# adaLN loads queued behind the weights' loads, and the attention masks built behind the layer's norm, in a four-stage decoder trunk

## The chip, the cores and the metric

One core of one Trainium2 chip runs the whole program. The metric is the device time in microseconds (us) of one execution; the profile is one execution of the same program, taken by the hardware profiler, and its span runs from the first to the last instruction. The engines are TensorE (PE, whose weight loads are listed as PEld), VectorE (DVE), ScalarE (ACT), GpSimd (POOL) and SyncE (SP, which here only issues DMAs).

## The reference

The trunk has two residual layers of 1024 tokens by 1024 channels, in float32. Each layer is a mixer and then a gated MLP with a causal convolution (ConvFFN), and each of these is preceded by an RMS norm that is shifted, scaled and gated from a conditioning vector `c` (adaLN):

```
cs = silu(c)
for i in range(2):
    sh_m, sc_m, g_m, sh_f, sc_f, g_f = split(cs @ ada_w[i] + ada_b[i], 6)
    hm = rms_norm(x, norm_mix[i]) * (1 + sc_m) + sh_m
    y = even_mixer(hm) if i == 0 else odd_mixer(hm)
    x = x + g_m * y
    hf = rms_norm(x, norm_ffn[i]) * (1 + sc_f) + sh_f
    x = x + g_f * conv_ffn(hf)
```

The even mixer is a gated DeltaNet in four heads beside a multi-scale pooling. The odd mixer is attention in three groups (dilations 1, 4 and 16) with eight heads each: `q`, `k` and `v` come from one projection, `q` and `k` are normed, and the scores get an ALiBi bias and a causal window before the softmax.

## The kernel before

All large products are made three times over: a float32 operand `a` is split into a rounded part `hi` (a cast on ACT, L193) and its rest `lo = a - hi` (a subtraction, L194), and TensorE adds up `hi*hi`, `hi*lo` and `lo*hi` (L220 to L222 and L1442 to L1444). `granule` (L196) does that for one 128x512 block of weights: an SP DMA into a `raw` tile (four buffers), the cast to `whi`, and the rest to `wlo` (nine buffers each). Who makes the rest is the variable `lo_eng`: GpSimd or VectorE. `last_w` holds the last weights' DMA traced so far.

The program is written as generators. A dense one (`dense`, `update`, `units`) yields matmuls; a chain of small work is woven into it (`weave`, L92) at given distances. The framework then lists the traced instructions on each engine: it puts first what was traced first among what is ready by its own plan, and an instruction whose buffer or input isn't free yet may be passed by later ones. `after(ins)` (L109) adds the condition that the block's instructions on the engine of `ins` come behind `ins` in that engine's queue; those on other engines are not bound. Each engine then runs its queue strictly in order, and SP issues its DMAs in order too.

The stages, in us of the profiled span: the even mixer until about 450, its output projection and the norm of the first ConvFFN until about 606; ConvFFN 0 until about 1216 (its up projection to about 950 by a Strassen scheme, `up`, one block of 128 gate and value columns at a time, with weights loaded as 512 KB `wr` tiles by `w_sums`, L1296; then the down projection, `update`); the attention layer until about 2250; ConvFFN 1 to the end.

The adaLN products are not made on TensorE, but for a few at the start: `ada_steps` (L274) loads one 128x512 block of `ada_w` at a time into a `raw` tile (L278), multiplies it by a column of `cs` and adds it up on DVE (L292, L294) or, in the down projection, on ACT and POOL (L288, L290). It is advanced one step at a time by `step_back` (L115), which `units`, `update` and `up` call behind their matmuls. Steps run only where `secs_due` lets them: from the third head of the even mixer on (L792), where sections 4 to 9 are made, and then in ConvFFN 0 from its fifth block on (L1353), where the other 14 follow; `sections(24)` (L1371) finishes the rest before the attention layer's norm vector.

The attention layer `odd` starts with the spill of `xt`, sets `lo_eng` to VectorE, builds the masks (`bm`, `bd`, from `rel` and `par`) and the vector `gq`, and then runs `dense`: `section(g, "v", hq)` loads the first eight granules of weights, and `tproj` multiplies them with the normed tokens, 256 at a time. At that point only the first half of the tokens is normed. The norm of the second half is woven into the first `tproj` (L1525): four transposes and a sum (`sums_of`, L328), the reciprocal root on DVE (`rsqrt`, L130), a broadcast by TensorE (`row_of`, L377), and then eight tiles scaled (L394), shifted (L403, L404), cast (L406) and split (L407; the even tiles' rest by GpSimd, the odd ones' by VectorE; `last_norm` is the last of them, on VectorE). The masks are first read by the attention's scores, `gq` by the first turn of `q` (L1485).

Of the kernel before, what the change touches and what calls it, by code (L numbers as in the profile page):

```python
# [13 lines left out]
ALU = mybir.AluOpType  # L14
# [3 lines left out]
P = 128  # L18
T = 1024
D = 1024  # L20
KT = D // P
TT = T // P
HALF = 512
# [11 lines left out]
def trunk(ctx, tc, x, c, ada_w, ada_b, norm_mix, norm_ffn, ev_w_in, ev_w_out, gdn_conv_w,  # L35
# [35 lines left out]
    def t2k():  # L71
        return tmp("t2k", [P, HALF], 8)
# [19 lines left out]
    def weave(chain, dense):  # L92
        for need in chain:
            if callable(need):
                while not need():
                    assert next(dense) is not None or need()
                continue
            t = 0.0
            while t < need:
                c = next(dense, None)  # L100
                if c is None:
                    break
                t += c
# [5 lines left out]
    def after(inst):  # L109
        return tc.issue_after(inst.ins) if inst is not None else nullcontext()  # L110
# [73 lines left out]
    def colv(name, i, n=1):  # L184
        a = col_at[name] + i
        return cols[:, a:a + n]
# [87 lines left out]
    def ada_steps(l, secs, raw_of):  # L274

        def load(s, k):
            raw = raw_of()
            nc.sync.dma_start(raw, ada_w[l].rearrange("(p k) n -> p k n", k=KT)[:, k, s * P:s * P + HALF])  # L278
            return raw

        for s in secs:
            acc = tmp("ada_acc", [P, HALF], 2, pl=pa[0])
            raw = load(s, 0)
            yield 1
            for k in range(KT):
                nxt = load(s, k + 1) if k < KT - 1 else None
                if by_pool[0]:
                    nc.scalar.activation(raw if k else acc, raw, AF.Copy, scale=cs[:, k:k + 1])  # L288
                    if k:
                        nc.gpsimd.tensor_tensor(out=acc, in0=acc, in1=raw, op=ALU.add)  # L290
                elif k == 0:
                    nc.vector.tensor_scalar(out=acc, in0=raw, scalar1=cs[:, 0:1], scalar2=None, op0=ALU.mult)  # L292
                else:
                    nc.vector.scalar_tensor_tensor(out=acc, in0=raw, scalar=cs[:, k:k + 1], in1=acc,  # L294
                                                   op0=ALU.mult, op1=ALU.add)
                raw = nxt
                yield 1
            ada_cols(l, s, acc)
            yield 1
# [1078 lines left out]
    def odd(xt, h, vec, acc):  # L1378
# [1 line left out]
        gate = mod[1][:, 16:24]  # L1380
        ready, res, qks, vss = set(), {}, {}, {}
        spill(xs[1], xt)
        lo_eng[0] = nc.vector
        with tc.tile_pool(name="po", bufs=1) as po:
            fill(po, 64)

            def et(tag, bufs, shape=(P, HALF), dt=F32):
                return tmp(tag, shape, bufs, dt, pl=po)


            bm = po.tile([P, 3, P], F32, name="bm")
            bd = po.tile([P, P], F32, name="bd")
            rel = t2k()[:, :P]
            nc.gpsimd.iota(rel, pattern=[[1, P]], base=0, channel_multiplier=-1,
                           allow_small_or_imprecise_dtypes=True)
            for i in (0, 2):
                nc.gpsimd.affine_select(out=bm[:, i, :], in_=rel, compare_op=GE, fill=NEG, base=0,
                                        pattern=[[-1, P]], channel_multiplier=1)
            par = po.tile([P, 2], F32, name="par")
            nc.vector.tensor_reduce(out=par, in_=ident.rearrange("p (m s) -> p s m", s=2), axis=mybir.AxisListType.X,  # L1400
                                    op=ALU.add)
            nc.vector.tensor_scalar(out=par, in0=par, scalar1=NEG, scalar2=None, op0=ALU.mult)
            for s in range(2):
                ev = "p (m s) -> p s m"
                nc.vector.tensor_scalar(out=bd.rearrange(ev, s=2)[:, s, :], in0=bm[:, 0, :].rearrange(ev, s=2)[:, s, :],
                                        scalar1=0.5, scalar2=par[:, 1 - s:2 - s], op0=ALU.mult, op1=ALU.add)
            nc.gpsimd.tensor_scalar(out=rel, in0=rel, scalar1=-float(P), scalar2=None, op0=ALU.add)
            nc.gpsimd.affine_select(out=bm[:, 1, :], in_=rel, compare_op=GE, fill=NEG, base=0,
                                    pattern=[[1, P]], channel_multiplier=-1)
            gq = po.tile([P, 1], F32, name="gq")  # L1410
            nc.vector.scalar_tensor_tensor(out=gq, in0=colv("att_q", 0), scalar=float(P) ** -0.5, in1=colv("att_k", 0),
                                           op0=ALU.mult, op1=ALU.mult)

            def tok_rows(d, g, blk):
                if g == 0:
# [6 lines left out]
            def section(g, kind, i):  # L1422

                base, out_ = g * 3072, []
                for k in range(KT):
                    rows = w[k * P:(k + 1) * P, :]
                    if kind == "v":
                        out_.append(granule(rows[:, base + 2048 + i * HALF:base + 2048 + (i + 1) * HALF]))
                    else:
                        out_.append(granule(rows[:, base:base + 2048].rearrange("p (s c) -> p s c", s=2)  # L1430
                                            [:, :, i * 256:(i + 1) * 256], ("p (s c) -> p s c", dict(s=2))))
                return out_
# [82 lines left out]
            def dense():  # L1515
                for i, (g, hp) in enumerate(todo):
                    while i >= 2 and ("att", i - 2) not in ready:
                        yield None
                    hq = hp // 2
                    if (g, hq) not in vd:  # L1520
                        wg = section(g, "v", hq)
                        for b2 in range(4):
                            gen = tproj(wg, b2)
                            if i == 0 and b2 == 0:
                                weave(norm(xt, vec, h, 1, acc, (1.8, 4.5)), gen)  # L1525
                            while True:
                                try:
                                    c = next(gen)
                                except StopIteration as e:
                                    ps = e.value  # L1530
                                    break
                                if turn:
                                    run_turn(1)
                                yield c
                            v = big(F32, "v")
                            nc.scalar.copy(v, ps)
                            if b2 == 0:
                                vd[(g, hq)] = dram.tile([T, HALF], F32, name=f"vd{g}{hq}")
                            nc.gpsimd.dma_start(vd[(g, hq)][b2 * 256:(b2 + 1) * 256].rearrange("(i p) c -> p i c", p=P),
                                                v.rearrange("p (i c) -> p i c", i=2))  # L1540
                    load_values(i)
                    wg = section(g, "qk", hp)
                    for b2 in range(4):
                        gen = tproj(wg, b2)
                        while True:
                            try:
                                c = next(gen)
                            except StopIteration as e:
                                ps = e.value
                                break  # L1550
                            if turn:
                                run_turn(1)
                            yield c
                        turn.append([10, i, b2, qk_norm(ps)])
                with tc.issue_after(last_w[0].ins):
                    res["x"] = reload(xs[1])
                o = [[granule(osp2[i][:, s]) for s in HS] for i in range(2)]
                for ks in ((0, 1), (2, 3)):
                    upd = update(row_blocks(od_w_out[0], ks), o, gate, res["x"], BY_TILE, wide=True)
                    for n, c in enumerate(upd):  # L1560
                        if turn:
                            run_turn(1)
                        if n == 4 and ks[0] == 0:
                            o = [from_dram(osp2[i]) for i in (2, 3)]
                        yield c
                while ("half", 3) not in ready:
                    yield None
                lo_eng[0] = nc.gpsimd
                acc2, tl, n = edge_start(row_blocks(od_w_out[0], (4, 5, 6, 7)), res["m2"] + res["m3"], gate, res["x"], xs[3])
                for _ in range(n):  # L1570
                    yield next(tl)
                res["edge"] = acc2, tl
# [246 lines left out]
```

## Time and profile before

| | |
|---|---|
| median of 3 runs (lowest to highest) | 3010.16 us (3009.04 to 3019.13) |
| the profiled execution's own time | 3011.75 us |
| its span | 3009.6 us |
| mean granted TensorE clock | 0.992 |
| PE busy | 2957.1 us (98%), 14386 matmuls |
| DVE busy | 1937.1 us (64%) |
| ACT busy | 1122.9 us (37%) |
| POOL busy | 980.7 us (33%) |

Busy times of different engines overlap, so they don't add up to the span. A row of a timeline gives the start, the busy time, the engine, the line, the operation, the tiles written and read, and how many like it were merged; in brackets stands how long the engine had been idle before it, and what it waited for. A row without brackets followed its predecessor without a pause. The columns of the stretches are named with their group.

### The profile page before, as it was taken

What the parts mean: (1) busy time and instruction counts of PE and PEld (TensorE: products, weight loads), DVE (VectorE), ACT (ScalarE), POOL (GpSimd) and SP (SyncE); (2) the same over time, 40 slices, a digit from 0 to 9 for tenths busy, and PEclk for the clock granted to TensorE, in tenths of its full rate; (3) what the DMA queues carried; (4) which work ended last, traced back from release to release, by engine and by line L of the source; (5) the groups of instructions that cost most, each with busy time, mean ns of one, the idle gap of its engine ahead of it and who ended that gap; (6) DMA issues with size and microseconds to landing.
All of it is one profiled execution on the core that took longest, in us unless ns stands there. A gap on an engine that the chain in (4) does not pass through costs nothing. (4 is left out here: it accounts for less than half of the span.)

```text
span 3009.6 us, 40263 instructions
## 1 busy us (share of the span) xinstructions
PE 2957.1 (98%) x14386; PEld 2445.2 (81%) x14386; DVE 1937.1 (64%) x3800; ACT 1122.9 (37%) x2237; POOL 980.7 (33%) x781
## 2 busy tenths in 40 slices
PE   7999999999999999999999999999999999999999
PEld 5878777888888888788888888888877788888888
DVE  6677756898886566554445646463687777676554
ACT  5433433533334433434233333333344433333210
POOL 4222312565556864200000010100002555556540
PEclk9999999999999999999999999999999999999999
DMA  8123343254344653412223232323153322224321
GB/s 272 45 84 87 91 144 109 88 164 129 118 133 143 207 157 117 149 36 92 76 78 109 71 125 67 126 64 114 59 188 112 91 85 84 85 85 161 116 88 57
DMA packets 270211, 331.47 MB, mean 110 GB/s; under 512 B 27219, under 2 KB 188090, under 8 KB 270010
## 3 DMA queue, kind: packets, MB, share of 16 engines
q1 hardware_dynamic: 259706, 294.15, 31.1%
q0 software_dynamic: 9344, 31.56, 3.2%
q10 hardware_dynamic: 960, 3.18, 0.3%
q8 instruction: 114, 1.87, 0.3%
q14 instruction: 87, 0.71, 0.1%
HBM read 251.82 MB, written 77.00 MB: 109 GB/s over the span
## 5 line engine op out<-in xcount | busy, mean ns | idle before, releaser
L1442 PE MATMUL mm<-whi,hh 128*128 128x512 f32 x1152 | 482.4, 419 | 0.0
L1444 PE MATMUL mm<-whi,hl 128*128 128x512 f32 x1152 | 452.5, 393 | 0.0
L1443 PE MATMUL mm<-wlo,hh 128*128 128x512 f32 x1152 | 450.8, 391 | 0.0
L194 POOL TENSOR_TENSOR wlo<-raw,whi 128x512 fp32r<-128x512 f32 x174 | 233.8, 1360 | 521.6 <-ACT whi L193 335.8
L254 DVE SCALAR_TENSOR_TENSOR xr<-sp,mod,xr 128x512 f32<-128x512 f32 x336 | 251.3, 750 | 183.9 <-PE sp L222 183.2
L193 ACT ACTIVATE whi<-raw 128x512 fp32r<-128x512 f32 x342 | 213.2, 629 | 302.1 <-PE sp L221 107.6
L220 PE MATMUL mm<-hh,whi 128*128 128x512 f32 x768 | 310.2, 405 | 9.6 <-ACT whi L193 3.8
L220 PE MATMUL sp<-oh,whi 128*128 128x512 f32 (+1 forms) x832 | 312.5, 376 | 0.0
L221 PE MATMUL mm<-hl,whi 128*128 128x512 f32 x768 | 307.0, 400 | 3.6 <-POOL hl L407 1.9
L222 PE MATMUL sp<-oh,wlo 128*128 128x512 f32 (+1 forms) x832 | 310.2, 373 | 0.0
L221 PE MATMUL sp<-ol,whi 128*128 128x512 f32 (+1 forms) x832 | 310.1, 373 | 0.0
L222 PE MATMUL mm<-hh,wlo 128*128 128x512 f32 x768 | 304.4, 396 | 0.1
L194 POOL TENSOR_TENSOR wlo<-t2k,whi 128x512 fp32r<-128x512 f32 x152 | 218.0, 1448 | 150.0 <-ACT whi L193 110.7
L1444 PEld LDWEIGHTS mm<-whi,hl 128*128 128x128 f32 x1152 | 216.2, 188 | 48.0
L1443 PEld LDWEIGHTS mm<-wlo,hh 128*128 128x128 f32 x1152 | 217.5, 189 | 37.0
L1442 PEld LDWEIGHTS mm<-whi,hh 128*128 128x128 f32 x1152 | 217.1, 188 | 35.8
L194 POOL TENSOR_TENSOR wlo<-wr,whi 128x512 fp32r<-128x512 f32 x108 | 169.0, 1566 | 160.6 <-ACT whi L193 154.7
L220 PEld LDWEIGHTS mm<-hh,whi 128*128 128x128 f32 x768 | 146.3, 191 | 41.0 <-issue 5.4
L222 PEld LDWEIGHTS sp<-oh,wlo 128*128 128x128 f32 x832 | 156.7, 188 | 27.6
L220 PEld LDWEIGHTS sp<-oh,whi 128*128 128x128 f32 x832 | 156.7, 188 | 27.1
L221 PEld LDWEIGHTS sp<-ol,whi 128*128 128x128 f32 x832 | 156.8, 188 | 26.8
L221 PEld LDWEIGHTS mm<-hl,whi 128*128 128x128 f32 x768 | 146.7, 191 | 34.1 <-POOL hl L407 4.4
(395 smaller groups left out, 5991.1 us busy)
## 6 DMA issues: line engine op xcount, KB each, us to landing
raw<-in_ada_w_dram SPq DMA_DIRECT2D x160, 256.0 KB
wr<-in_ffn_w_up_dram SPq DMA_DIRECT2D x72, 512.0 KB
raw<-in_od_w_in_dram SPq DMA_DIRECT2D x144, 256.0 KB
hid<-ft SPq DMA_DIRECT2D x44, 512.0 KB
raw<-in_ffn_w_down_dram SPq DMA_DIRECT2D x88, 256.0 KB
big<-hid SPq DMA_DIRECT2D x44, 512.0 KB
xr<-xs SPq DMA_DIRECT2D x32, 512.0 KB
os<-stg SPq DMA_DIRECT2D x96, 130.0 KB
```

The costliest lines, as they stand in the source:

```text
L193: nc.scalar.activation(dst_hi, src, AF.Copy)
L194: eng.tensor_tensor(out=dst_lo, in0=src, in1=dst_hi, op=ALU.subtract)
L220: nc.tensor.matmul(ps, wh, mh, start=first, stop=False)
L221: nc.tensor.matmul(ps, wh, ml, start=False, stop=False)
L222: return nc.tensor.matmul(ps, wl, mh, start=False, stop=last)
L254: nc.vector.scalar_tensor_tensor(out=xt[o][:, s], in0=p, scalar=gate[:, o:o + 1], in1=xt[o][:, s], op0=ALU.mult, op1=ALU.add)
L1442: nc.tensor.matmul(p, hh, wh, start=(k == 0), stop=False)
L1443: nc.tensor.matmul(p, hh, wl, start=False, stop=False)
L1444: nc.tensor.matmul(p, hl, wh, start=False, stop=(k == KT - 1))
```

## The change

Two places change. In `ada_steps`, every DMA of `ada_w` is now bound behind the last weights' DMA that was traced before it. In `odd`, `lo_eng` stays GpSimd until the first section of weights has been traced, and the masks and `gq` are built by a function `tables`, which is called when the norm of the second half has been traced; its VectorE instructions are bound behind the norm's last one, its GpSimd instructions have no such bond.

```diff
         def load(s, k):
             raw = raw_of()
-            nc.sync.dma_start(raw, ada_w[l].rearrange(...)[:, k, s * P:s * P + HALF])
+            with after(last_w[0]):
+                nc.sync.dma_start(raw, ada_w[l].rearrange(...)[:, k, s * P:s * P + HALF])
             return raw
...
         spill(xs[1], xt)
-        lo_eng[0] = nc.vector
         with tc.tile_pool(name="po", bufs=1) as po:
...
             bm = po.tile([P, 3, P], F32, name="bm")
             bd = po.tile([P, P], F32, name="bd")
-            rel = t2k()[:, :P]
-            nc.gpsimd.iota(rel, ...)
-            (two affine_select, one tensor_scalar and one affine_select on gpsimd,
-             one tensor_reduce, three tensor_scalar and one scalar_tensor_tensor on vector)
             par = po.tile([P, 2], F32, name="par")
             gq = po.tile([P, 1], F32, name="gq")
+
+            def tables():
+                rel = t2k()[:, :P]
+                nc.gpsimd.iota(rel, ...)
+                (the same instructions in the same order)
...
                     if (g, hq) not in vd:
                         wg = section(g, "v", hq)
+                        lo_eng[0] = nc.vector
                         for b2 in range(4):
                             gen = tproj(wg, b2)
                             if i == 0 and b2 == 0:
                                 weave(norm(xt, vec, h, 1, acc, (1.8, 4.5)), gen)
+                                with after(last_norm[0]):
+                                    tables()
```

## Rows read from the trace of the kernel before

**Rows 1.** Stretches: us, busy (count) PE, PEld, DVE, ACT, POOL; clock, DMA, GB/s.
```profile
606.00:890.00 284.00, 283.62 (x1261) 234.88 (x1262) 246.91 (x285) 101.58 (x148) 157.32 (x106) 1.00 0.44 136
890.00:1222.00 332.00, 331.10 (x1484) 274.00 (x1482) 214.84 (x293) 137.40 (x193) 210.13 (x146) 1.00 0.50 158
199.00:206.00 7.00, 6.38 (x15) 4.60 (x16) 6.96 (x15) 2.34 (x4) 2.51 (x2) 0.53 0.64 180
```
**Rows 2.** Timeline of PE, at 199 and around the start of `odd`.
```profile
199.48 0.79 PE L220 MATMUL mm<-hh,whi 128*128 128x512 f32 x1 [3.76 <-ACT whi L193]
...
1215.50 0.39 PE L222 MATMUL sp<-oh,wlo 128*128 128x512 f32 x1
...
1222.21 0.66 PE L332 MATMUL sp<-ident,t2k 128*128 128x128 f32 x4 [1.11 <-DVE t2k L374]
...
1229.63 1.16 PE L381 MATMUL sp<-ident,rs 128*128 128x128 f32 x8 [1.05 <-DVE rs L140]
```
**Rows 3.** Timeline of SP's DMA queue in the even mixer.
```profile
88.76 0.37 SPq L198 DMA_DIRECT2D raw<-in_ev_w_in_dram  x1
94.22 22.10 SPq L278 DMA_DIRECT2D raw<-in_ada_w_dram  x4
...
195.61 1.16 SPq L198 DMA_DIRECT2D raw<-in_ev_w_in_dram  x2
```
**Rows 4.** Timeline of SP's DMA queue in ConvFFN 0's first blocks.
```profile
598.43 5.81 SPq L1296 DMA_DIRECT2D wr<-in_ffn_w_up_dram  x4
...
614.98 11.93 SPq L278 DMA_DIRECT2D raw<-in_ada_w_dram  x11
626.96 0.42 SPq L1296 DMA_DIRECT2D wr<-in_ffn_w_up_dram  x1
```
**Rows 5.** Timeline of DVE around the start of `odd`.
```profile
1202.56 0.69 DVE L194 TENSOR_TENSOR wlo<-raw,whi 128x512 fp32r<-128x512 f32 x1 [0.41 <-ACT whi L193]
...
1204.37 1.29 DVE L194 TENSOR_TENSOR wlo<-raw,whi 128x512 fp32r<-128x512 f32 x2
...
1206.57 1.34 DVE L194 TENSOR_TENSOR wlo<-raw,whi 128x512 fp32r<-128x512 f32 x1
...
1219.20 0.74 DVE L254 SCALAR_TENSOR_TENSOR xr<-sp,mod,xr 128x512 f32<-128x512 f32 x1
...
1222.27 1.04 DVE L1411 SCALAR_TENSOR_TENSOR gq<-cols 128x1 f32<-128x1 f32 x1
...
1226.04 0.68 DVE L333 TENSOR_REDUCE rs<-sp 128x4 f32<-128x512 f32 x1
1226.64 0.68 DVE L194 TENSOR_TENSOR wlo<-raw,whi 128x512 fp32r<-128x512 f32 x1
...
1254.65 0.69 DVE L194 TENSOR_TENSOR wlo<-raw,whi 128x512 fp32r<-128x512 f32 x1 [12.19 <-ACT whi L193]
```
**Rows 6.** Page, costliest groups: rests of weights on GpSimd (busy us, mean ns).
```profile
L194 POOL TENSOR_TENSOR wlo<-raw,whi 128x512 fp32r<-128x512 f32 x174 | 233.8, 1360 | 521.6 <-ACT whi L193 335.8
```
**Rows 7.** Two DVE lines in ConvFFN 0: ns min/median/max, first and last start.
```profile
L1313 DVE TENSOR_TENSOR t2k<-wr,wr x18: 676/938/1749, 611.1 to 931.5; 128x512 f32<-128x512 f32 x18
...
L1330 DVE TENSOR_TENSOR t2k<-t2k,mm x18: 674/687/690, 627.7 to 947.6; 128x512 f32<-128x512 f32 x18
```
**Rows 8.** Timeline of POOL around the start of `odd`.
```profile
1221.63 1.66 POOL L407 TENSOR_TENSOR hl<-t2k,hh 128x512 fp32r<-128x512 f32 x1 [1.56 <-DVE hh L406]
...
1241.33 0.97 POOL L1539 DMA_DIRECT2D vd<-v  x1
```
**Rows 9.** Timeline of ACT: last cast of the first section, first use of `gq`.
```profile
1217.32 0.62 ACT L193 ACTIVATE whi<-raw 128x512 fp32r<-128x512 f32 x1
...
1281.62 0.69 ACT L1485 ACTIVATE qkT<-sp,gq 128x512 f32<-128x512 f32 x1 [6.09 <-PE sp L1474]
```
**Rows 10.** What SP's queue waited for, 600 to 960: total us, times, longest.
```profile
SPq L1296 <- POOL wlo L194: 81.6, 27, 7.7
SPq L1296 <- DVE t2k L1313: 56.9, 16, 4.7
```

More of the change, by code (lines that the diff above doesn't have):

```diff
@@ L277, in load @@
             raw = raw_of()
-            nc.sync.dma_start(raw, ada_w[l].rearrange("(p k) n -> p k n", k=KT)[:, k, s * P:s * P + HALF])
+            with after(last_w[0]):
+                nc.sync.dma_start(raw, ada_w[l].rearrange("(p k) n -> p k n", k=KT)[:, k, s * P:s * P + HALF])
             return raw
@@ L1392, in odd @@
             bd = po.tile([P, P], F32, name="bd")
-            rel = t2k()[:, :P]
[L1394 to L1398, printed above, removed]
-            par = po.tile([P, 2], F32, name="par")
-            nc.vector.tensor_reduce(out=par, in_=ident.rearrange("p (m s) -> p s m", s=2), axis=mybir.AxisListType.X,
-                                    op=ALU.add)
@@ L1402, in odd @@
[L1402 to L1407, printed above, removed]
@@ L1408, in odd @@
-            nc.gpsimd.affine_select(out=bm[:, 1, :], in_=rel, compare_op=GE, fill=NEG, base=0,
-                                    pattern=[[1, P]], channel_multiplier=-1)
-            gq = po.tile([P, 1], F32, name="gq")
-            nc.vector.scalar_tensor_tensor(out=gq, in0=colv("att_q", 0), scalar=float(P) ** -0.5, in1=colv("att_k", 0),
-                                           op0=ALU.mult, op1=ALU.mult)
+            par = po.tile([P, 2], F32, name="par")
+            gq = po.tile([P, 1], F32, name="gq")
@@ new lines, in tables @@
+            def tables():
+                rel = t2k()[:, :P]
+                nc.gpsimd.iota(rel, pattern=[[1, P]], base=0, channel_multiplier=-1,
+                               allow_small_or_imprecise_dtypes=True)
+                for i in (0, 2):
+                    nc.gpsimd.affine_select(out=bm[:, i, :], in_=rel, compare_op=GE, fill=NEG, base=0,
+                                            pattern=[[-1, P]], channel_multiplier=1)
+                nc.vector.tensor_reduce(out=par, in_=ident.rearrange("p (m s) -> p s m", s=2), axis=mybir.AxisListType.X,
+                                        op=ALU.add)
+                nc.vector.tensor_scalar(out=par, in0=par, scalar1=NEG, scalar2=None, op0=ALU.mult)
+                for s in range(2):
+                    ev = "p (m s) -> p s m"
+                    nc.vector.tensor_scalar(out=bd.rearrange(ev, s=2)[:, s, :], in0=bm[:, 0, :].rearrange(ev, s=2)[:, s, :],
+                                            scalar1=0.5, scalar2=par[:, 1 - s:2 - s], op0=ALU.mult, op1=ALU.add)
+                nc.gpsimd.tensor_scalar(out=rel, in0=rel, scalar1=-float(P), scalar2=None, op0=ALU.add)
+                nc.gpsimd.affine_select(out=bm[:, 1, :], in_=rel, compare_op=GE, fill=NEG, base=0,
+                                        pattern=[[1, P]], channel_multiplier=-1)
+                nc.vector.scalar_tensor_tensor(out=gq, in0=colv("att_q", 0), scalar=float(P) ** -0.5, in1=colv("att_k", 0),
+                                               op0=ALU.mult, op1=ALU.mult)
```

## The prediction, made before the changed kernel ran

> **What bounds the kernel now.** I read the stretches first, then the waits of PE, then the queues of the two places that change. From 606 to 890 PE is busy for 283.62 of 284 us and from 890 to 1222 for 331.10 of 332, at full clock [rows 1]. So in ConvFFN 0, which holds all adaLN loads whose order can change (below), there is 1.28 us to win in 616 us, and 0.90 of that belongs to one gap that PE's timeline shows from 1221.10 to 1222.21: 1.11 us, waiting for DVE's sum of squares. A second gap, of 1.05 us ahead of the broadcast at 1229.63, waits for DVE's reciprocal root [rows 2]. Both stand where `odd` starts, and together they are 2.16 us. The reader is to see that everything else which the change touches runs beside a TensorE that is never short of work, so a gain is a shorter gap of PE there, and a loss is a new one. What can be told apart by measuring this kernel I take as 0.3%, 9.0 us of 3010.16.
>
> **The adaLN loads.** The bond matters only where a load stood ahead of a weights' DMA traced before it. In the even mixer none did: the code traces 18 weights' loads ahead of the first adaLN step, the 18th is at 88.76, and the first four adaLN loads follow at 94.22 [rows 3]. The next weights' pair, at 195.61, is traced behind them and stays behind them; `raw` has four buffers and both kinds of load use them in the order of the trace. The same holds in the down projection. So the 3.76 us for which PE waits at 199.48 [rows 2], because four adaLN blocks hold all `raw` tiles from 94 to 194, stays. In ConvFFN 0 the `wr` tiles come from another pool, and there adaLN loads do run ahead: eleven of them are issued from 614.98 on, ahead of a `wr` at 626.96 that the code traces before most of them [rows 4]. Of the 160 adaLN loads some 57 lie there (seven sections of eight and one more, counted in the code), and most will be issued some us to some ten us later. Cost: each is one DMA issue on SP that only changes its place; the `wr` loads and the stores of `hid` that it stood ahead of go no later than before. The DVE work is the same number of multiply-adds, later by the same time. I take 0. What hides it: PE is fed one block ahead, and DVE is idle for 284 - 246.91 = 37.1 us of the 284 [rows 1], 2.5 us in each block (a block is seven products of 12 matmuls; 1261 matmuls in 284 us make 0.225 us each, so a block is 18.9 us and there are 15). Below zero it can't go by more than PE's idle time there, 0.38 us from 606 to 890. If the cover is gone it costs what the first rival says.
>
> **The first weights' rests.** Eight subtractions leave DVE and go to POOL. Four of them stood at 1202 to 1208 and took 0.69 + 1.29 + 1.34 = 3.3 us [rows 5]; the other four stood behind 1223 among the masks. First the second gap, which is the simpler one. The transposes for the sum end at 1222.21 + 0.66 = 1222.87 [rows 2], but DVE begins the reduction at 1226.04 without a pause before it, and then puts one more rest (0.68) ahead of the root [rows 5]. In these 3.17 us stand `gq` (1.04), three rests, `par`, `bd` and one rest of the norm (`hl`, 0.68 like the others of its kind). All but the last leave. So the root is ready 3.17 - 0.68 + 0.68 = 3.2 us earlier at best, against a gap of 1.05: the gap goes, with 2.1 us to spare. Bounds: 1.05 gained, or nothing if POOL holds up the small instructions of the root by more than 2.1 us; `gq`, with one element per partition, shows what such a hold is, 1.04 us beside a POOL instruction that ends at 1221.63 + 1.66 = 1223.29 [rows 5, 8].
>
> The first gap hangs on DVE's backlog. The last matmul of the layer ahead ends at 1215.89 [rows 2], and DVE comes to its result only at 1219.20, straight from other work [rows 5]: 3.3 us late. From there the square on ACT and the sum on DVE lead to the transposes at 1222.21. Taking 3.3 us out of DVE's queue before 1208 would close the gap by itself. But the rests are now made by POOL at the same time, and that is not free for DVE. A DVE instruction with both inputs in SBUF takes 676 ns at best, 938 at the median and 1749 at most; one whose second input is in PSUM takes 674 to 690 whatever POOL does [rows 7]. So one POOL instruction can hold one such DVE instruction by 0.26 us at the median and by 1.07 at most. Between 1202 and 1222 DVE has about ten of them (by the code four sums of squares, three rests of the norm and three casts), and POOL would be busy there for eight rests of 1.36 us [rows 6] that it didn't have before. Ten holds of 0.26 cost 2.6 us, nearly the 3.3 that were saved; none at all closes the gap, ten of 1.07 less 3.3 would widen it by 7.4. I take the value of the nearest row, the median: 3.3 - 2.6 = 0.7 us less backlog, a first gap of 0.4 instead of 1.11, and round the gain down to 0.5, since some holds are there already.
>
> The Trainium skill ("SBUF — State Buffer", section "Who interferes with whom") says that GpSimd and a VectorE instruction with two SBUF inputs share a read interface, and that the later one waits for all of the earlier. The trace agrees in that the holds reach 1.07 us, nearly a POOL instruction's 1.36, and that inputs from PSUM are never held; it differs in that the median hold is a fifth of one. Taken at its word for every pair, the rule turns the gain of 0.5 into a loss, which is the second rival.
>
> POOL itself must not come late. The last cast of the section ends at 1217.94 [rows 9]; even if the second four rests and two rests of the norm all came after it, at 1.36 to 1.66 us each [rows 6, 8], POOL would be done at 1226.1 to 1227.9. DVE delivered the last rest at 1226.64 + 0.68 = 1227.3 [rows 5] and PE never waited for it. I take 0, with 0.6 us lost at the far end.
>
> **The masks.** About 2 us of POOL and some 1.5 us of DVE move behind the norm, to about 1242. On DVE they are bound behind its last instruction; the next one there comes at 1254.65 after 12.19 us of idle time [rows 5], which hides them. On POOL they fall beside its issue of the stores of `v`, at 1241.33 [rows 8]; were they ahead of it, that store would be 2 us later, and the values are read back only when three more have followed. `gq` is first read at 1281.62 [rows 9] and the masks after that. I take 0, and 2 us of POOL's time, none of PE's, if the order is bad.
>
> **The sum.** The profiled execution took 3011.75 us (span 3009.6 and 2.15 around it). Less 1.05 and 0.5 that is 3010.2. The median of the runs is 1.59 us below the profiled execution, so the forecast is 3008.6 us, 0.05% less than before: no change that can be measured. The parts' bounds give 3008.0 (both gaps gone) to about 3015 (second rival).
>
> **Rivals.**
> (1) *The adaLN loads hold up VectorE; slower.* A load now stands behind a `wr` that waits for its buffer, and SP is in order. The `wr` loads waited 81.6 + 56.9 = 138.5 us in 43 waits, 3.2 us each, 7.7 at most [rows 10]. If DVE comes to a multiply-add whose block isn't there, everything behind it in DVE's queue waits, also the additions that empty PSUM. A block has 2.5 us of idle DVE time [rows 1]; from the point at which the wait in a block is longer than that, PE pays. One wait of 3.2 per block costs 0.7 x 16 blocks = 11 us: 3020; two cost (6.4 - 2.5) x 16 = 62 us: 3071. For it: DVE is 87% busy in this stretch. Against it: DVE's own additions of `wr` tiles stand behind the same DMAs, and neither they nor PE wait visibly now.
> (2) *POOL takes the port from VectorE in the first gap.* Six two-input instructions held by 1.07 us more make 6.4 us, less 3.3 saved: the first gap grows by 3.1 to 4.2. The gap of 3.76 at 199.48 was followed by a stretch of 7 us at a granted clock of 0.53 [rows 1, 2], the lower of the two levels, 1.2 GHz, where half of the work is lost, 3.3 us. Together with the second gap's 1.05: 3.1 + 3.3 - 1.05 = +5.4, 3015.5. For it: POOL is nearly without a pause there. Against it: the median hold.
> (3) *Both gaps go.* 2.16 us: 3008.0.
> (4) *The change reaches the even mixer.* If the plan did put the weights of 195.61 ahead of the first four adaLN loads, the 3.76 us and about 3.3 us of low clock behind it would go as well: 3008.6 - 7.1 = 3001.5. Against it: the order of the trace above.
> (5) *It doesn't do what it says:* the queues come out as before, or the first section's rests are already cast too late to matter: 3010.2.
>
> **How the numbers follow.** Forecast 0.45; (1) 0.08; (2) 0.17; (3) 0.15; (4) 0.06; (5) 0.09. The forecast's own range is 3007 to 3011. The forecast, (3) and (5) lie within 2.2 us of each other, less than the three runs differ among themselves (3009.0 to 3019.1), so the range is set by (2), (4) and that spread: 3002 to 3018 holds all but (1), most of (4) and a little of the rest. Faster than 3001.1: half of (4) and a few hundredths for an order that I don't foresee, 0.06. Slower than 3019.2: (1) and a little of (2), 0.10. No change: 0.84.
>
> **What would show it.** Right: no gap of PE ahead of the broadcast near 1229, the reduction on DVE directly behind its transposes, eight rests on POOL between 1202 and 1224, the masks behind 1240, and in ConvFFN 0 every adaLN load behind a `wr`, with PE still at 99.8%. Wrong: a wait of DVE for `raw` in ConvFFN 0 with PE gaps behind it; a gap ahead of the transposes that is longer than 1.11; a moved order of loads before 450; a stretch at low clock after 1200.

## The result, and the profile after

The changed kernel takes 3017.86 us (median of 19 runs, 3012.58 to 3023.72), the kernel before 3011.48 us on the same chips (19 runs, 3004.84 to 3019.13): a ratio of 1.0020, 95% interval 1.0013 to 1.0028. That is 6 us slower (3.9 to 8.4). The forecast was 1.6 us faster; the time is just inside its range and the direction is wrong.

The profiled execution of after is a long one, 3023.72 us with a span of 3022.0, 12.4 us over the span of before. Where these 12.4 us lie is seen when both traces are cut at the same matmuls: at the 1st, the 2501st, the 3201st, the 5501st and the 5901st. The stretches of before (us, then busy time and count of PE, PEld, DVE, ACT and POOL, then clock, DMA share and GB/s) are the even mixer, ConvFFN 0 and the start of `odd`:

```profile
4.30:510.90 506.60, 476.25 (x2501) 377.84 (x2502) 346.49 (x768) 204.51 (x490) 131.81 (x132) 0.97 0.39 120
669.50:1184.90 515.40, 515.40 (x2302) 426.81 (x2301) 372.33 (x457) 196.81 (x278) 325.47 (x218) 1.00 0.47 146
1184.90:1275.50 90.60, 88.43 (x401) 72.96 (x400) 53.31 (x103) 39.66 (x58) 22.09 (x25) 1.00 0.39 130
```

and the same matmuls in after, with the surroundings of its one gap in the last three lines:

```profile
4.40:518.50 514.10, 482.21 (x2500) 381.51 (x2501) 346.68 (x768) 204.36 (x490) 131.62 (x132) 0.96 0.38 118
677.10:1192.50 515.40, 515.40 (x2301) 426.79 (x2301) 379.55 (x460) 196.61 (x277) 327.94 (x219) 1.00 0.46 149
1192.50:1287.40 94.90, 90.57 (x401) 74.86 (x400) 52.25 (x96) 39.78 (x58) 31.55 (x32) 0.96 0.37 125
...
1222.00:1230.80 8.80, 6.29 (x28) 4.88 (x26) 8.70 (x13) 6.39 (x11) 5.54 (x5) 1.00 0.59 211
1230.80:1237.60 6.80, 4.98 (x14) 4.11 (x15) 4.93 (x16) 1.63 (x2) 1.22 (x1) 0.50 0.33 113
1237.60:1245.00 7.40, 7.40 (x37) 6.22 (x37) 5.04 (x9) 4.32 (x7) 2.38 (x2) 1.00 0.00 0
```

ConvFFN 0 is as long as before. The start of `odd` is 4.2 us longer, though PE's work there is the same. The other 0.7 us lie outside these three stretches. The even mixer is 7.5 us longer, but there the change moves nothing: the order of all queues up to 592 us is that of before. The table of all ten profiles, below, shows that this stage differs as much between kernels that share that order. So 4.2 us is what the trace gives to the change, inside the interval of 3.9 to 8.4.

PE's timeline of after has, for the two gaps of [rows 2], these lines (start, busy, and in brackets the idle time and what it waited for):

```profile
1223.14 0.39 PE L222 MATMUL sp<-oh,wlo 128*128 128x512 f32 x1
...
1232.62 1.11 PE L333 MATMUL sp<-ident,t2k 128*128 128x128 f32 x4 [4.33 <-DVE t2k L375]
...
1238.87 1.05 PE L382 MATMUL sp<-ident,rs 128*128 128x128 f32 x8
```

The first gap grew from 1.11 to 4.33 us, and a stretch of 6.8 us at a granted clock of 0.50 (1.2 GHz) begins inside it; the second gap is gone. DVE's timeline of after in the same stretch, which answers to [rows 5]:

```profile
1210.61 0.69 DVE L395 TENSOR_TENSOR t2k<-xr,sp 128x512 f32<-128x512 f32 x1 [0.82 <-PE sp L382]
1211.22 0.88 DVE L375 TENSOR_TENSOR t2k<-t2k,t2k 128x512 f32<-128x512 f32 x1
1212.55 0.98 DVE L407 CAST hh<-t2k 128x512 fp32r<-128x512 f32 x1 [0.46 <-issue]
...
1214.95 1.75 DVE L375 TENSOR_TENSOR t2k<-t2k,t2k 128x512 f32<-128x512 f32 x1 [0.17 <-ACT t2k L374]
...
1219.41 1.41 DVE L375 TENSOR_TENSOR t2k<-t2k,t2k 128x512 f32<-128x512 f32 x1
...
1224.98 1.82 DVE L375 TENSOR_TENSOR t2k<-t2k,t2k 128x512 f32<-128x512 f32 x1
...
1227.32 0.74 DVE L254 SCALAR_TENSOR_TENSOR xr<-sp,mod,xr 128x512 f32<-128x512 f32 x1
1227.98 1.75 DVE L194 TENSOR_TENSOR wlo<-raw,whi 128x512 fp32r<-128x512 f32 x1
...
1231.19 1.37 DVE L375 TENSOR_TENSOR t2k<-t2k,t2k 128x512 f32<-128x512 f32 x1
1233.77 0.69 DVE L334 TENSOR_REDUCE rs<-sp 128x4 f32<-128x512 f32 x1 [1.21 <-PE sp L333]
```

POOL's timeline of after, which answers to [rows 8]:

```profile
1210.25 1.29 POOL L194 TENSOR_TENSOR wlo<-raw,whi 128x512 fp32r<-128x512 f32 x1 [29.25 <-ACT whi L193]
1211.84 1.41 POOL L194 TENSOR_TENSOR wlo<-raw,whi 128x512 fp32r<-128x512 f32 x1 [0.29 <-ACT whi L193]
...
1214.85 3.00 POOL L194 TENSOR_TENSOR wlo<-raw,whi 128x512 fp32r<-128x512 f32 x2
...
1224.95 4.23 POOL L194 TENSOR_TENSOR wlo<-raw,whi 128x512 fp32r<-128x512 f32 x3
...
1247.21 0.24 POOL L1399 IOTA t2k<- 128x128 f32 x1
```

Read them in pairs. The sum of squares (L375) takes 0.68 us alone. The one at 1214.95 starts 0.10 us behind a POOL rest and takes 1.75; the one at 1224.98 starts 0.03 behind one and takes 1.82; the rest at 1227.98 stands beside the three of 1224.95 and takes 1.75. Each is held for most of one POOL instruction. Held are also the sum of 1211.22, by 0.20, the sums of 1219.41 and 1231.19, which stand beside POOL's rests of the norm, and the cast of 1212.55 (0.98, 0.41 alone), which reads only one tile of SBUF. In the same stretch of before, DVE's timeline has two sums held beside POOL's rests of the norm:

```profile
1211.88 1.41 DVE L374 TENSOR_TENSOR t2k<-t2k,t2k 128x512 f32<-128x512 f32 x1
...
1217.45 1.23 DVE L374 TENSOR_TENSOR t2k<-t2k,t2k 128x512 f32<-128x512 f32 x1
```

How that makes 4.33 out of 1.11:

- DVE comes to the layer's last product at 1227.32, 3.79 us behind the end of PE's last matmul of it (1223.14 + 0.39 = 1223.53); before it was 3.3. Four rests were taken off DVE: 3.32 us by [rows 5], 3.07 from start to start, since each record reaches some 0.08 us into the next. But DVE then stood idle for 0.82 + 0.46 + 0.17 = 1.45 us, against 0.41 in before [rows 5], and was held for 0.20 + 0.57 + 1.07 + 0.73 + 1.14 = 3.71 us, against 0.73 + 0.55 = 1.28. 1.04 + 2.43 - 3.07 = 0.40 us more backlog instead of less; 0.48 measured.
- From there to the transposes it takes 1232.62 - 1227.32 = 5.30 us instead of 1222.21 - 1219.20 = 3.01: a rest of the *next* section now stands ahead of the last sum (1.75, held), and that sum is held too (1.37 instead of 0.68). 2.29 us.
- PE asks 0.45 us earlier: from the layer's last matmul to the gap it has 4.76 us of other work, 5.21 before, two matmuls less.

0.48 + 2.29 + 0.45 = 3.22 = 4.33 - 1.11. With PE's work of 4.98 us in the stretch at half speed (2.5 us lost) and the second gap's 1.05 off, that is 3.2 + 2.5 - 1.05 = 4.7 us, against 4.2 measured.

The adaLN loads did move: on SP's queue, in place of [rows 4], the loads now come in fours behind the `wr` loads.

```profile
606.07 5.73 SPq L1297 DMA_DIRECT2D wr<-in_ffn_w_up_dram  x4
611.85 3.33 SPq L279 DMA_DIRECT2D raw<-in_ada_w_dram  x4
...
623.58 6.53 SPq L1297 DMA_DIRECT2D wr<-in_ffn_w_up_dram  x2
630.20 1.96 SPq L279 DMA_DIRECT2D raw<-in_ada_w_dram  x4
```

### The profile page after: what moved, and what is told of

It reads as the page before. It is cut to its first block, busy times and chain, and to the rows that moved or that the text cites. A ratio compares the mean times of both kernels' runs of the same rounds, so it can differ in the third digit from the quotient of the medians.

```text
span 3022.0 us, 40256 instructions
## 1 busy us (share of the span) xinstructions
PE 2963.2 (98%) x14386; PEld 2447.9 (81%) x14386; DVE 1938.6 (64%) x3792; ACT 1123.3 (37%) x2237; POOL 994.0 (33%) x789
## 5 line engine op out<-in xcount | busy, mean ns | idle before, releaser
L194 POOL TENSOR_TENSOR wlo<-raw,whi 128x512 fp32r<-128x512 f32 x182 | 245.1, 1363 | 554.3 <-ACT whi L193 361.7
```

Of the source, the lines that this page charges most:

```text
L194: eng.tensor_tensor(out=dst_lo, in0=src, in1=dst_hi, op=ALU.subtract)
```

## The experiments

The ten profiles by stage, each cut at the same matmuls, in us. The half clock of the even mixer is the sum of the stretches at the lower clock behind 150 us, that of `odd` the one that begins in the gap.

| kernel | even mixer | its half clock | ConvFFN 0 | start of `odd` | gaps there | half clock there |
|---|---|---|---|---|---|---|
| before | 506.61 | 23.9 | 515.35 | 90.68 | 1.11, 1.05 | none |
| after | 514.11 | 34.1 | 515.37 | 94.90 | 4.33 | 6.8 |
| e1, loads | 510.82 | 30.7 | 515.35 | 90.70 | 1.11, 1.08 | none |
| e2, masks | 504.67 | 20.5 | 515.35 | 90.82 | 1.04, 1.28 | none |
| e3, rests | 504.97 | 20.5 | 515.37 | 94.60 | 3.56 | 6.8 |
| e4, masks and rests | 505.95 | 20.5 | 515.35 | 94.73 | 4.33 | 6.8 |
| e5, POOL writes only | 504.61 | 17.1 | 516.47 | 89.69 | 0.99 | none |
| e6, PE asks later | 507.15 | 20.5 | 515.37 | 88.27 | none | none |
| e7, masks, PE asks later | 505.33 | 20.5 | 515.35 | 89.22 | 0.91 | none |
| e8, even weights first | 513.56 | 30.7 | 515.37 | 90.68 | 1.10, 1.07 | none |

The first four take the change apart: each is the kernel before with one part of it.

**e1, the bond of the adaLN loads alone.**

```diff
-            nc.sync.dma_start(raw, ada_w[l].rearrange(...)[:, k, s * P:s * P + HALF])
+            with after(last_w[0]):
+                nc.sync.dma_start(raw, ada_w[l].rearrange(...)[:, k, s * P:s * P + HALF])
```

> The kernel before with the bond of the adaLN loads alone. PE's queue comes out the same as before. Theory 1 (POOL's rests hold VectorE where odd starts): 0 us, both gaps there as before (1.1 and 1.05 us), PE without a gap in ConvFFN 0's blocks. Theory 2 (the new order of the queues at the start of odd, not the port): 0 us too. Theory 3 (the adaLN loads, issued behind the weights', make VectorE late): this run carries the loss, +4 to +8 us, with new gaps of PE between 606 and 1222.

Measured: 3011.99 us against 3010.52, ratio 1.0003 (0.9993 to 1.0013). ConvFFN 0 takes 515.35 us, as in before, and the start of `odd` 90.70. The bond costs nothing that the trace or the runs show; that theory falls.

**e2, the masks behind the norm alone.** `tables` as in the change, `lo_eng` set to VectorE where it was.

```diff
+                                with after(last_norm[0]):
+                                    tables()
```

> The kernel before with the masks alone moved behind the norm; the first section's rests stay on VectorE, no bond on the adaLN loads. PE's broadcast comes out one place (four matmuls) earlier, the rest of PE's queue is the same. Theory 1: the first gap stays at about 1.1 us, the second goes or shrinks to under 0.5; no stretch at low clock at the start of odd; -0.5 to -1 us. Theory 2: the second gap doesn't shrink, since PE asks earlier; 0 us.

Measured: 3010.03 us, ratio 0.9999 (0.9989 to 1.0008). The masks cost nothing that the runs can tell. But the second gap didn't shrink, though its cause, DVE's small work ahead of the root, is gone. PE's timeline of e2:

```profile
1220.21 0.66 PE L332 MATMUL sp<-ident,t2k 128*128 128x128 f32 x4 [1.04 <-DVE t2k L374]
1227.18 1.16 PE L381 MATMUL sp<-ident,rs 128*128 128x128 f32 x8 [1.28 <-DVE rs L140]
```

DVE's timeline of e2 between them:

```profile
1220.08 2.37 DVE L194 TENSOR_TENSOR wlo<-raw,whi 128x512 fp32r<-128x512 f32 x2
...
1223.58 0.68 DVE L333 TENSOR_REDUCE rs<-sp 128x4 f32<-128x512 f32 x1
```

In the place of that small work stand rests, directly behind the last sum, one of them held (2.37 for two). So the root is ready only 0.45 us earlier after the transposes than in before, and the plan put PE's broadcast three matmuls (0.7 us) nearer to them. Most of the time that the edit frees is filled by the plan, and PE is told to ask earlier.

**e3, the first rests on GpSimd alone.**

```diff
-        lo_eng[0] = nc.vector
...
                         wg = section(g, "v", hq)
+                        lo_eng[0] = nc.vector
```

> The kernel before with the first section's rests alone on GpSimd; masks where they were, no bond on the adaLN loads. Theory 1: VectorE's sums of squares beside POOL take up to 1.8 us instead of 0.7, the first gap grows from 1.1 to about 4 us and a stretch at half clock of about 7 us follows; +3 to +5 us. Theory 2: here VectorE has no rest of the next section ahead of the last sum, so the first gap stays under 2.5 us, no half clock; 0 to +1 us.

Measured: 3014.65 us, ratio 1.0015 (1.0006 to 1.0023). PE's row of e3:

```profile
1222.13 1.12 PE L332 MATMUL sp<-ident,t2k 128*128 128x128 f32 x4 [3.56 <-DVE t2k L374]
```

The stretch of e3 behind it, columns as above:

```profile
1221.00:1227.80 6.80, 5.67 (x16) 4.62 (x17) 5.78 (x21) 1.62 (x2) 3.28 (x6) 0.52 0.44 154
```

One line moved makes nearly the whole loss: 3.9 us at the start of `odd`, and a gap of 3.56. DVE's backlog at the layer's end is that of after, 3.80 us, with three sums held at 1.74, 1.41 and 1.83 us. Ahead of the last sum, a rest of the next section stands here too, but not held (0.68), and that sum isn't either (0.68), for POOL's last three rests are done by then. With `gq`, which stands there in e3, the way from the layer's last product to the transposes takes 4.06 us instead of 5.30, and PE asks 0.46 us earlier: 4.33 - 1.24 + 0.46 = 3.55.

**e4, masks and rests.** Both edits, without the bond.

> The whole change without the bond of the adaLN loads. Theories 1 and 2: as the whole change, a first gap of about 4.3 us, half clock for about 7 us behind it, no second gap; +4 us against before. Theory 3: as before, or better by 1 us.

Measured: 3016.13 us, ratio 1.0017 (1.0006 to 1.0027); 94.73 us and a gap of 4.33, as in after.

**e5, POOL writes without reading.** The whole change, but the first section's rests are not computed: POOL writes zeros in their place (the first lines are in `split`, which makes the cast and the rest).

```diff
+        if blank[0]:
+            nc.gpsimd.memset(dst_lo.bitcast(F32), 0.0)
+            return
...
+                        blank[0] = (g, hq) == (1, 0)
                         wg = section(g, "v", hq)
+                        blank[0] = False
```

> The whole change, but the eight rests of the odd layer's first weights are replaced by GpSimd writes of zeros that read no SBUF: this leaves out the rests of that one section. GpSimd stays about as busy and PE, VectorE and ScalarE keep the order of instructions of the changed kernel. Theory 1 (GpSimd's reads of SBUF hold VectorE's instructions with two SBUF inputs, and the held sums arrive late): the sums beside GpSimd fall from 1.4 to 1.8 us towards 0.7 us, the gap ahead of the transposes falls from 4.33 to under 1.5 us and no stretch at half clock follows; the stretch from the first matmul of the last third of ConvFFN 0's end to the odd layer's fourth hundredth matmul takes about 90.5 us instead of 94.90. Theory 2 (the new order of the queues alone, with the next section's rest ahead of the last sum, makes the gap): the gap stays at 3.5 to 4.5 us and the half clock behind it too, 94 to 95 us.

Measured: 3007.1 us in a single execution, too little for a comparison of times; the trace is what counts here. The queues of PE, DVE and ACT are those of after to the last instruction, the next section's rest ahead of the last sum included. POOL's timeline of e5:

```profile
1213.28 0.53 POOL L197 MEMSET wlo<- 128x512 f32 x1 [2.73 <-PE sp L227]
...
1215.40 0.98 POOL L197 MEMSET wlo<- 128x512 f32 x2
...
1219.11 1.29 POOL L413 TENSOR_TENSOR hl<-t2k,hh 128x512 fp32r<-128x512 f32 x1 [2.72 <-DVE hh L412]
```

DVE's timeline of e5:

```profile
1213.48 0.60 DVE L412 CAST hh<-t2k 128x512 fp32r<-128x512 f32 x1
...
1215.43 0.69 DVE L380 TENSOR_TENSOR t2k<-t2k,t2k 128x512 f32<-128x512 f32 x1
...
1219.54 1.40 DVE L380 TENSOR_TENSOR t2k<-t2k,t2k 128x512 f32<-128x512 f32 x1
```

PE's timeline of e5:

```profile
1221.00 0.66 PE L338 MATMUL sp<-ident,t2k 128*128 128x128 f32 x4 [0.99 <-DVE t2k L380]
```

The sum at 1215.43 stands beside two POOL writes and is not held; the one at 1219.54 stands beside a POOL subtraction and is. The cast of 1213.48 is held even beside a write, by 0.19. With the order of after and without POOL's reads for these eight, DVE's backlog at the layer's end is 1.39 us instead of 3.79, the gap is 0.99, no half clock follows, and the broadcast waits 0.21: the holds make the loss, not the order. A limit of this run is that the writes are also shorter (0.5 us) and earlier, since they wait for no cast, and the next section's loads were issued earlier for it; so it doesn't say how much of 4.2 us is reading and how much is the longer stay; the pair of sums does show that writes don't hold a sum. ConvFFN 0 is 1.1 us longer in e5, part of it a wait of PE for POOL of 0.53 at 1126.4 that no other profile has; the start of `odd` is counted from behind it.

The Trainium skill ("SBUF — State Buffer", section "Who interferes with whom") says just this: a VectorE instruction with two SBUF inputs contends with a GpSimd instruction that reads SBUF and not with one that only writes it. The trace agrees, 0.69 against 1.40 us.

**e6, PE asks later.** The whole change, with the norm woven into the first two products of `odd` at wider distances: the transposes stand 21 matmuls further down PE's queue than in after, the broadcast 27. `blocks` yields the products of the listed parts of the tokens one behind the other and stores each as before.

```diff
...
-                                weave(norm(xt, vec, h, 1, acc, (1.8, 4.5)), gen)
...
+                        runs = [blocks((0, 1)), blocks((2, 3))] if i == 0 else [blocks(range(4))]
+                        for gen in runs:
+                            if i == 0 and gen is runs[0]:
+                                weave(norm(xt, vec, h, 1, acc, (9.0, 4.5)), gen)
...
```

> The whole change, but the norm is woven into the first two transposing products of the odd layer instead of the first one, with waits of 9.0 and 4.5 us: on PE the transposes of the sum stand some 22 matmuls (22 x 0.225 = 5 us) later and the broadcast some 27 later. If the loss is only that PE asks for the sums before VectorE, held by GpSimd, can have them: no gap of PE over 0.3 us at either place, no half clock, the stretch at the start of the odd layer about 88.6 us (90.68 before, less both gaps of 1.11 and 1.05), and the time about 2 us under the kernel before, ratio 0.999 to 1.000. Rival (the held VectorE loses throughput and not only delay, so the gap comes back at the later place or at the eviction of PSUM): the stretch stays over 91.5 us.

Measured: 3008.50 us against 3009.99, ratio 0.9992 (0.9981 to 1.0004). The stretch of e6 that held the gaps, columns as above:

```profile
1215.00:1245.00 30.00, 30.00 (x139) 24.69 (x138) 24.34 (x44) 18.33 (x27) 16.48 (x16) 1.00 0.30 106
```

PE's timeline of e6, the same two instructions, with no wait in brackets:

```profile
1226.06 0.60 PE L333 MATMUL sp<-ident,t2k 128*128 128x128 f32 x4
...
1231.28 1.05 PE L382 MATMUL sp<-ident,rs 128*128 128x128 f32 x8
```

The start of `odd` takes 88.27 us, 6.6 less than after and 2.4 less than before, with DVE held as in after (three of its sums take 1.74, 1.39 and 1.82 us, its backlog at the layer's end is 3.78). So the holds cost nothing by themselves: what costs is that PE asks before DVE can have the sums. This version beats the changed kernel (their intervals against the kernel before don't overlap); against the kernel before the gain is that of the trace, and the runs alone don't settle it.

**e7, masks behind the norm, rests on VectorE, PE asks later.** As e6, with distances of 6.8 and 6.8 and without the bond.

> The masks behind the norm as in the change, the first rests on VectorE as before, the adaLN loads as before, and the norm woven into two products with waits of 6.8 and 6.8 us: transposes some 10 matmuls (2.3 us) and the broadcast some 18 (4 us) later than before. Theory (both gaps are a matter of where PE's queue asks): both go, 90.68 - 1.11 - 1.05 = 88.5 us at the start of the odd layer, ratio 0.9993. Rival (the plan fills the freed time of VectorE with other work, and the gap moves with the place): a gap of about 1 us stays at one of the two places, 89.6 us.

Measured: 3008.57 us, ratio 0.9993 (0.9984 to 1.0003); 89.22 us. Both gaps went, and one of 0.91 came at a third place, for a rest that DVE now makes too late (PE's timeline of e7):

```profile
1222.64 0.50 PE L1446 MATMUL mm<-wlo,hh 128*128 128x512 f32 x1 [0.91 <-DVE wlo L194]
```

The rival was right in kind: on a loaded DVE a wait of about 1 us stays, though at a place that it didn't name. In e6 POOL makes those rests, and there is none. That suggests that the move of the rests is of use once PE's place is right; it isn't shown, since e6 and e7 differ in their distances too.

**e8, the even mixer's weights ahead of its adaLN loads.** The forecast's fourth rival, made on the kernel before: the adaLN steps begin one unit later.

```diff
-                    if hd == 2:
-                        secs_due[0] = 10
...
+                    if hd == 2:
+                        secs_due[0] = 10
```

> The kernel before, with the even mixer's adaLN steps begun one unit later, so that the weights' loads that stood behind the first four adaLN loads are issued ahead of them. For the mechanism that the forecast named as its fourth rival (four adaLN blocks hold all raw tiles from 94 to 194 us, PE then waits 3.76 us at 199.48 for the weights, and half clock follows): that gap goes and so does the half clock behind it, 3.8 + 3.3 = about 7 us off the even mixer's 506.6, ratio 0.998. Rival (PE is only fed later, or the even mixer's length is set by what differs from run to run there, 504.7 to 514.1 us with one and the same queue): no difference that the rounds can tell, ratio 0.999 to 1.001.

Measured: 3011.89 us, ratio 1.0006 (0.9995 to 1.0017). The gap of 3.76 [rows 2] is gone, and PE has no gap of over 0.3 us between 81 and 205 us. But the next one is new, in PE's timeline of e8:

```profile
208.12 1.42 PE L1104 MATMUL sp<-ident,o 128*128 128x128 f32 x6 [2.25 <-DVE o L1091]
```

So PE waits for DVE some nine us later instead, and the stage takes 513.56 us. PE's idle time from 30 to 520 is 27.9 us, 25.9 in before. The runs show no gain, as the rival named ahead of them had it; what sets this stage's length stays open, and since the order of PE's queue differs behind the old gap too, the run doesn't price that gap by itself.

## Why the prediction was wrong

**What bounds the kernel** held: PE's feed decides, and the change could only act through the gaps at the start of `odd`.

**The adaLN loads**: right. The even mixer's order is unchanged, ConvFFN 0 is as long, e1 shows 1.0003. Rival (1) didn't come.

**The second gap**: gone as forecast in after, but without the "2.1 us to spare". The root is ready at 1237.31 and PE reaches the broadcast at 1238.87, after 15 matmuls that ran at half clock for the most part; e5, with the same queue at full clock, waits 0.21 there. So the change itself shrinks the second gap to some 0.2 us, as far as e5 can stand for it, and that nothing of it is left in after is luck: the loss at the first gap slowed PE. In e2 the gap even grew. The step took PE's place in its queue as fixed, and the plan put the broadcast nearer to the transposes in each kernel with one of these edits (26 places behind the last of them in before, 23 in e2, 17 in e3, 16 in e4, after and e5). One detail of the count was wrong too: the last rest in [rows 5] ahead of the root, at 1226.64, was of the next section, so it didn't leave DVE, and the plan put it ahead of the last sum.

**The first gap** is the step that failed: "Ten holds of 0.26 cost 2.6 us ... I take the value of the nearest row, the median". The holds in after are 5.5 us in seven instructions, 0.78 each (0.20, 0.57, 1.07, 0.73, 1.14, 1.07, 0.69), 4.2 more than the 1.28 of before. The median of L1313 in [rows 7] was not the nearest row. Nine of its 18 instructions met a POOL instruction and took 1.19 to 1.75 us; the other nine met none and took 0.68 or 0.69. The median, 938 ns, lies midway between one that met none and the shortest that met one (DVE's timeline of before):

```profile
630.79 0.69 DVE L1313 TENSOR_TENSOR t2k<-wr,wr 128x512 f32<-128x512 f32 x1
...
662.83 1.19 DVE L1313 TENSOR_TENSOR t2k<-wr,wr 128x512 f32<-128x512 f32 x1
```

So no instruction was held by 0.26; the nine that met one were held by 0.77 on average, and the bound of 1.07 was the hold of one that began 0.1 us behind a POOL instruction, which is what happens where POOL runs two and three rests back to back. The count of ten was off as well: from 1202 to 1222 DVE has six sums, three rests of the norm and four casts, of which some met POOL and some didn't.

Three more terms of the first gap stood at nothing in the sum: 1.04 us more in which DVE stood idle with the rests gone, the next section's rest that the plan put ahead of the last sum (1.75, held), and PE asking 0.45 us earlier. The half clock, which only rival (2) had, came with the longer gap. With that, two of the forecast's signs of being wrong are there: a gap ahead of the transposes of more than 1.11, and a stretch at low clock after 1200.

**Rival (2)** had the mechanism and nearly the size: a gap of 4.2 forecast, 4.33 measured; half clock with it, 6.8 us; +5.4 forecast, +4.2 by the trace and +6.0 (3.9 to 8.4) by the runs. That its gap came out so near is in part luck: its holds were too long (6.4 us, 5.5 measured), it let all of the 3.3 us of rests count as saved, and it lacked the next section's rest and PE's earlier place. Its price for the low clock, 3.3 us, was too high, since 1.8 of the 6.8 us fell into the gap itself. "Against it: the median hold" was the wrong argument. The sentence that the rule of the Trainium skill "differs in that the median hold is a fifth of one" was no difference at all: the rule speaks of instructions that meet, and half of those behind the median met none.

**POOL not late, and the masks**: right; the masks' POOL work begins at 1247.21, and e2 shows no cost.

**The profile of after** would have shown a loss of 12.4 us to someone who compares spans; 7.5 of it is the even mixer, whose order the change doesn't touch.

## What to carry to other kernels

When work moves to GpSimd beside a VectorE that makes something the next stage waits for, count the VectorE instructions with two SBUF inputs that will meet it, and price each by those that met one (here 0.7 to 1.1 us beside a GpSimd instruction of 1.3 us, less where it was nearly done), not by a median that also counts those that met none. Casts belong to the count: one with a single SBUF input was held too. Then look at where the consumer asks: the same held VectorE cost 4 us with the transposes at their place and nothing with them 5 us later. And compare two traces stage by stage, cut at the same matmuls, before a difference of spans is put down to a change.

## What was not expected of the hardware

A wait of 4.33 us (3.56 in e3) came with 6.8 us at half clock, which began inside it, while the waits of about 1 us in the same place came with none in any of the profiles.

A cast that reads one tile of SBUF, 0.41 us alone, took 0.98 beside a subtraction on GpSimd and 0.60 beside a write of zeros (e5), while a sum with two SBUF inputs took 0.69 beside such writes.

The even mixer takes 504.6 to 514.1 us in ten profiles, nine of them with one and the same order of its queues. The long ones show more half clock (34.1 us in after, 30.7 in e1) than the short ones (17.1 to 20.5). What makes one execution fall into more such stretches than another was not found, and e8 shows that removing its largest single wait behind 150 us doesn't settle it.
